# Second tiles moved straight behind gate and up, rows turned ahead of down, second rows always fetched

## The chip, the cores and the metric

The kernel runs on one core of one Trainium2 chip. The metric is the device time of one execution in microseconds (us); of several executions the median is given. TensorE (PE) does the matrix products and transposes, VectorE (DVE) and ScalarE (ACT) the element work, GpSimd (POOL) issues the gathers and the adding scatters, and SyncE (SP) issues most of the weight loads. DMA engines move data beside them.

## The reference

One encoder layer over 1024 tokens of width 1024: a token mixer (neighbourhood attention beside a bidirectional gated DeltaNet, one output projection), and then a mixture of 64 small experts. The change touches the experts alone. Each token chooses one of 8 groups and in it the 2 best of 8 experts; each expert's hidden width is 256.

```python
def expert_block(args):
    tok, e = args
    xb = h_pad[tok]
    hid = jax.nn.silu(xb @ w_gate[e]) * (xb @ w_up[e])
    return hid @ w_down[e]
...
out = (out.reshape(p_rows, d_).astype(jnp.float32) * buf_gate[:, None]).astype(h.dtype)
y = jnp.zeros((n + 1, d_), h.dtype).at[buf_tok].add(out)[:n]
```

All weights are float32: 2 MB for gate and up of one expert, 1 MB for down, 201 MB for all 64. Which tokens an expert gets is known only at run time.

## The kernel before, in words

The mixer, the router and the tables of rows take the first 840 us or so. The experts follow, in 32 steps of two experts each (e and e + 32). Each expert gives a first tile of up to 64 rows, so that a step fills 128 rows. An expert with more than 64 tokens has a second tile of up to 64 rows, which is computed only if it is there.

Step i of the loop (lines 1145 to 1168) consists of these pieces, written in this order:

- weights: `load_w` (L951, its DMA is L958) for the tiles that come free. There are 7 tiles of gate and up (`wg`) and 6 of down (`wd`). At step 0 these loads are on POOL's queue, later on SP's.
- `gather` (L1019) of the 128 rows of step i + 2 into one of three buffers `xg`, an indirect DMA issued by POOL (L1021). In this program's lists the three buffers are xg_8037, xg_8038 and xg_8039, for steps 0, 1 and 2, then 3, 4 and 5, and so on.
- `gate_up` (L1034): 16 products into `pp` on PE (L1041; the trace counts two matmuls for each, 32 in all), SiLU on ACT (L1044), the product with up on DVE into `sg` (L1045).
- the branch on the larger count of the two experts (L1155): when it is taken, the second rows `xs` are turned and one `second_tile` (L1081) is done for each expert that has one (inner branch L1159, its sum into the output is L1057 too).
- `second` (L1125) for the next step: its count is loaded into registers of all engines (L1127), and inside a branch of its own (L1128) the two gathers of second rows are issued.
- `finish(i - 1)`: `down` (L1066) of the step before: 8 products into `po` (L1076; 16 in the trace), the scaling on DVE (L1078), and an indirect DMA on POOL that adds the rows into the output (L1057).
- `turn_h` (L1048): two transposes of `sg`.
- `turn` (L1024) for the next step: 8 transposes of `xg` on PE (L1029), multiplied on DVE into `xT` (L1030).

A scheduler reorders the instructions of each engine within a stretch between two branches; it does not move them past a branch's ends. So what stands ahead of a branch in an engine's list stays ahead of it. The branch is decided by each engine for itself, from registers that it loads with TENSOR_LOAD. `reuse_waits="tile"` means that a tile's next writer waits for the last reader of the tile.

In this profile the branch L1155 is taken in 6 of the 32 steps, and 7 second tiles are done. The first is in step 0.

Of the kernel before, what the change touches and what calls it, by code (L numbers as in the profile page):

```python
# [8 lines left out]
F32 = mybir.dt.float32  # L9
# [10 lines left out]
P = 128  # L20
# [10 lines left out]
CAP = 64  # L31
# [5 lines left out]
def tile_layer(ctx, tc, a, out):  # L37
# [31 lines left out]
    def load_split(src, cols):  # L69
        hi = wpl.tile([P, NK, 256], F32R, name="w_hi")[:, :, :cols]  # L70
        lo = wpl.tile([P, NK, 256], F32R, name="w_lo")[:, :, :cols]
        for k in range(0, NK, 2):
            raw = wpl.tile([P, 2, 256], F32, name="w_raw")[:, :, :cols]
            sp.dma_start(raw, src[:, k:k + 2])
            act.activation(hi[:, k:k + 2], raw, AF.Copy)  # L75
            dve.tensor_sub(lo[:, k:k + 2], raw, hi[:, k:k + 2].bitcast(F32))  # L76
        return hi, lo
# [352 lines left out]
    ws = {b: load_split(a["w_nat"][b], 256) for b in border[:2]}  # L430
# [33 lines left out]
    with tc.tile_pool(name="ty", bufs=1, side="right") as ty:  # L464
        TT = ty.tile([P, NH, CH], F32, name="TT")
        XdT = ty.tile([P, NH, 32], F32, name="XdT")
        wt = ty.tile([P, NH, 32], F32, name="wt")
# [42 lines left out]
    for n in range(NCH):  # L510
# [3 lines left out]
        at, w = atb[n % 2], wb[n % 2]  # L514
# [450 lines left out]
    steps = [(gp, gp * 8 + j) for j in range(8) for gp in range(4)]  # L965
    wt = {}
    pace = [steps[i // 2][1] + 32 * (i % 2) for i in range(4)]
    for f, t in [(None, 0)] + tail:
        ins = f(t) if f else last
        if f is None or f is ao_mm and t in (4, 6, 7):  # L970
            e = pace.pop(0)
            wt.setdefault(e % 32, []).append(load_w(mwA, e, after=ins))
        if f is ao_mm and t == NT - 1:
# [5 lines left out]
            tS = [m1.tile([P, 32, 4], I32, name="tS"), m1.tile([CAP, 64, 4], I32, name="t2")]  # L979
            ln2p = m1.tile([P, NK], F32, name="ln2p")  # L980
            act.dma_start(ln2p, a["ln2"][:, 1])
            LA = 2
            xgb = [m1.tile([P, D], F32, name=f"xg{i}") for i in range(LA + 1)]
            xg2 = m1.tile([P, D], F32, name="xs")
# [31 lines left out]
    psX = ctx.enter_context(tc.tile_pool(name="psX", bufs=2, space=PSUM, reuse_waits="tile"))  # L1016
# [3 lines left out]
    def gather(xg, meta, n):  # L1020
        return pool.indirect_dma_start(out=xg[:n], out_offset=None, in_=x2_d, in_offset=bass.IndirectOffsetOnAxis(ap=meta[:n, 0:1], axis=0),  # L1021
                                bounds_check=S - 1, oob_is_err=False)

    def turn(xg, n):  # L1024
        xT = m2.tile([P, NK, P], F32, name="xT")
        for g in range(2):
            pt = psX.tile([P, 4, P], F32, name="pt")
            for k in range(4):
                pe.transpose(pt[:, k, :n], xg[:n, g * 4 + k:D:NK], ident[:n, :n])  # L1029
            dve.tensor_tensor(xT[:, g * 4:g * 4 + 4, :n], pt[:, :, :n],  # L1030
                              ln2p[:, g * 4:g * 4 + 4, None].to_broadcast([P, 4, n]), op=OP.mult)
        return xT

    def gate_up(ws, meta, xT):  # L1034

        n = CAP * len(ws)
        mf = meta.bitcast(F32)
        pp = psX.tile([P, 2, 256], F32, name="pp")
        for k in range(NK):
            for d in range(len(ws)):  # L1040
                pe.matmul(pp[d * CAP:(d + 1) * CAP], xT[:, k, d * CAP:(d + 1) * CAP],  # L1041
                          ws[d][0][:, :, k * 256:(k + 1) * 256], start=(k == 0), stop=(k == NK - 1))
        sg = m2.tile([P, 256], F32, name="sg")
        act.activation(sg[:n], pp[:n, 0], AF.Silu, scale=mf[:n, 3:4])  # L1044
        dve.scalar_tensor_tensor(sg[:n], pp[:n, 1], mf[:n, 3:4], sg[:n], op0=OP.mult, op1=OP.mult)  # L1045
        return sg

    def turn_h(sg, n):  # L1048
        ph = psX.tile([P, 2, P], F32, name="ph", bufs=1)
        for k in range(2):  # L1050
            pe.transpose(ph[:, k, :n], sg[:n, k:256:2], ident[:n, :n])  # L1051
        hT = m2.tile([P, 2, P], F32, name="hT")
        act.activation(hT[:, :, :n], ph[:, :, :n], AF.Copy)  # L1053
        return hT
# [12 lines left out]
    def down(ws, meta, hT, gp):  # L1067
        n = CAP * len(ws)
        mf = meta.bitcast(F32)
        yg = m2.tile([P, D], F32, name="yg", bufs=3)  # L1070
        for c in range(2):
            cs = slice(c * 512, (c + 1) * 512)
            po = psX.tile([P, 512], F32, name="po")
            for k in range(2):
                for d, w in enumerate(ws):
                    pe.matmul(po[d * CAP:(d + 1) * CAP], hT[:, k, d * CAP:(d + 1) * CAP],  # L1076
                              w[1][:, k * D + c * 512:k * D + (c + 1) * 512], start=(k == 0), stop=(k == 1))
            dve.tensor_scalar(yg[:n, cs], po[:n], mf[:n, 2:3], None, op0=OP.mult)  # L1078
        add_rows(yg[:n], meta[:n, 0:1], gp, (0, 1))

    def second_tile(w, d, meta, xT, gp):  # L1081

        hs = [slice(0, CAP), slice(CAP, 2 * CAP)]
        me, mine = hs[0], hs[d]
        mf = meta.bitcast(F32)
        pp = psX.tile([P, 2, 256], F32, name="pp")
        for k in range(NK):
            for i in range(2):
                pe.matmul(pp[hs[i], i], xT[:, k, mine], w[0][:, i, k * 256:(k + 1) * 256], start=(k == 0), stop=(k == NK - 1))
        sg = m2.tile([CAP, 256], F32, name="sg2", bufs=1)  # L1090
        act.activation(sg[:], pp[me, 0], AF.Silu, scale=mf[me, 3:4])
        dve.scalar_tensor_tensor(sg[:], pp[hs[1], 1], mf[me, 3:4], sg[:], op0=OP.mult, op1=OP.mult)
        ph = psX.tile([P, 2, P], F32, name="ph", bufs=1)
        for k in range(2):
            pe.transpose(ph[:, k, :CAP], sg[:, k:256:2], ident[me, me])
        hT = m2.tile([P, 2, CAP], F32, name="hT2", bufs=1)
        act.activation(hT, ph[:, :, :CAP], AF.Copy)
        yg = m2.tile([P, D], F32, name="yg", bufs=3)
        po = psX.tile([P, 512], F32, name="po")
        for k in range(2):  # L1100
            for c in range(2):
                pe.matmul(po[hs[c]], hT[:, k], w[1][:, k * D + c * 512:k * D + (c + 1) * 512],
                          start=(k == 0), stop=(k == 1))
        for c in range(2):
            dve.tensor_scalar(yg[me, c * 512:(c + 1) * 512], po[hs[c]], mf[me, 2:3], None, op0=OP.mult)
        add_rows(yg[me], meta[me, 0:1], gp, (d,))

    NS = len(steps)
# [14 lines left out]
    more, xTs = {}, {}  # L1123

    def second(i):  # L1125
        e = steps[i][1]
        more[i] = nc.values_load(ci[:, e:e + 1], min_val=0, max_val=S)  # L1127
        with tc.If(more[i] > CAP):  # L1128
            for d in range(2):
                gather(xg2[d * CAP:(d + 1) * CAP], tS[1][:, e + 32 * d], CAP)  # L1130

    for i in range(LA):
        ins = gather(xgb[i], tS[0][:, steps[i][1]], P)
    for i in placed[-2:]:
        tc.add_manual_dep(i.ins, ins.ins.name, mybir.DependencyInfo(mybir.DependencyClass.NoSync, mybir.DependencyReason.DATA),
                          reason="the first rows are more urgent")
    xTs[0] = turn(xgb[0], P)
    second(0)
    hTs = {}

    def finish(i):
        gp, e = steps[i]
        down(wt[e], tS[0][:, e], hTs.pop(i), gp)

    for i in range(NS):
        gp, e = steps[i]
        args = (pool, ins, mybir.DependencyClass.NoSync) if i == 0 else ()
        for n, part in upto(i):
            f = steps[n // 2][1]
            mw = mwA if n % room[part] < 4 else mwB if n % room[part] == 4 else (mwG, mwD)[part]  # L1150
            wt.setdefault(f, [[], []])[n % 2] += load_w(mw, f + n % 2 * 32, *args, parts=(part,))
        if i + LA < NS:
            gather(xgb[(i + LA) % (LA + 1)], tS[0][:, steps[i + LA][1]], P)
        sg = gate_up(wt[e], tS[0][:, e], xTs.pop(i))
        with tc.If(more[i] > CAP):  # L1155
            xT = turn(xg2, P)
            for d in range(2):
                c = nc.values_load(ci[:, 128 + e + 32 * d:129 + e + 32 * d], min_val=0, max_val=S)
                with tc.If(c > CAP):  # L1159
                    second_tile(wt[e][d], d, tS[1][:, e + 32 * d], xT, gp)  # L1160
        if i + 1 < NS:
            second(i + 1)
        if i > 0:
            finish(i - 1)
        hTs[i] = turn_h(sg, P)
        if i + 1 < NS:
            xTs[i + 1] = turn(xgb[(i + 1) % (LA + 1)], P)
    finish(NS - 1)
    rest = nc.values_load(ci[:, 32:33], min_val=0, max_val=S)  # L1169
    with tc.If(rest > 0):  # L1170
        with tc.For_i(0, 64) as e:
            left = nc.values_load(ci[:, bass.ds(e + 64, 1)], min_val=0, max_val=14)
            with tc.For_i(0, left) as i:
                w = load_w(mwA, e)
                meta = m2.tile([P, 4], I32, name="meta")
                sp.dma_start(meta[:CAP], tbl[bass.ds(e * S + i * CAP + 2 * CAP, CAP)])
                gather(xgb[0], meta, CAP)
                down([w], meta, turn_h(gate_up([w], meta, turn(xgb[0], CAP)), CAP), None)


def layout(inputs):
# [64 lines left out]
```

## Time and profile before

| | |
|---|---|
| median of 3 runs | 1406.26 us (1401.35 to 1408.34) |
| profiled execution, own time | 1408.78 us |
| its span in the trace | 1407.0 us (1.8 us lie around it) |
| mean granted TensorE clock | 0.944 |
| busy: PE, DVE, ACT, POOL | 85%, 47%, 28%, 28% of the span |
| experts stage | from about 842 us to the end |
| SP queue's weight loads | 62 of 2 MB, 63 of 1 MB |

Times in the trace count from the span's start. The trace's views used are: busy time of each engine in a chosen stretch (windows), instructions in order of time (timeline), the DMA queues' packets, one line's instructions, and the list of waits. In a timeline row the bracket at the end says how long the engine was idle before the instruction and what ended that idle time. An engine name with a q (PEq, DVEq, SPq) is that engine's sequencer, which runs branches and register loads. The DMA share of a window is the mean busy share of the 16 DMA engines; it can come out a little over 1.

### The profile page before, as it was taken

How to read it: one execution, taken by the hardware profiler on the slowest of the kernel's cores; microseconds unless marked ns; L12 is line 12 of the kernel's file. 1: busy time of each engine (PE TensorE's matmuls, PEld its weight loads, DVE VectorE, ACT ScalarE, POOL GpSimd, SP SyncE). 2: the span in 40 equal slices, each digit the busy share in tenths (PEclk: the TensorE clock that was granted, in tenths of full speed). 3: DMA queues.
4: the chain of work that ended last, by engine and by line, in shares of the span. 5: the costliest groups of instructions: out<-in, count | busy, mean ns of one | idle time of the engine just before them, and what ended most of it. 6: DMA issues, size and time to landing. Idle time of an engine off the chain costs nothing. (4 is left out here: it accounts for less than half of the span.)

```text
span 1407.0 us, 20840 instructions
## 1 busy us (share of the span) xinstructions
PE 1194.1 (85%) x7307; PEld 828.0 (59%) x7308; DVE 660.1 (47%) x1631; ACT 393.9 (28%) x800; POOL 387.4 (28%) x435
## 2 busy tenths in 40 slices
PE   6977999979999996688989968888887788878885
PEld 6866889969988895466768853333332333333332
DVE  5556853853667652667858871212211212222211
ACT  6435422322354441765445320000000000000000
POOL 1147313021655544112110242212212112211111
PEclk9989999989999997799999979999998899989998
DMA  4251246346565469998694788999999899998991
GB/s 158 71 114 42 75 135 177 94 138 148 166 176 148 119 172 221 297 262 206 169 216 165 285 332 323 397 404 401 400 406 394 352 387 407 395 364 331 402 379 38
DMA packets 109953, 347.11 MB, mean 247 GB/s; under 512 B 43104, under 2 KB 49248, under 8 KB 93168
## 3 DMA queue, kind: packets, MB, share of 16 engines
q1 hardware_dynamic: 74480, 260.68, 51.3%
q0 software_dynamic: 27056, 68.79, 19.0%
q10 hardware_dynamic: 8272, 15.78, 3.2%
q8 instruction: 82, 1.34, 0.4%
q14 instruction: 63, 0.52, 0.1%
HBM read 305.26 MB, written 61.67 MB: 261 GB/s over the span
## 5 line engine op out<-in xcount | busy, mean ns | idle before, releaser
L1041 PE MATMUL pp<-wg,xT 128*64 128x512 f32 x1024 | 233.1, 604 | 19.7 <-DVE xT L1030 19.4
L1041 PEld LDWEIGHTS pp<-wg,xT 128*64 128x64 f32 x1024 | 74.4, 139 | 156.4 <-issue 128.2
L1076 PE MATMUL po<-wd,hT 128*64 128x512 f32 x512 | 126.8, 622 | 45.1 <-DVEq L1155 28.3
L84 PE MATMUL pA<-w_hi,h_hi 128*128 128x256 f32 x512 | 151.1, 295 | 0.0
L86 PE MATMUL pA<-w_hi,h_lo 128*128 128x256 f32 x512 | 149.9, 293 | 0.0
L85 PE MATMUL pA<-w_lo,h_hi 128*128 128x256 f32 x512 | 149.9, 293 | 0.0
L1057 POOL DMA_INDIRECT out<-yg,tS x32 | 50.8, 1587 | 291.3 <-DVE yg L1078 242.8
L1045 DVE SCALAR_TENSOR_TENSOR sg<-pp,tS,sg 128x256 f32<-128x256 f32 x32 | 15.5, 484 | 233.2 <-ACTq L1155 189.0
L1076 PEld LDWEIGHTS po<-wd,hT 128*64 128x64 f32 x512 | 42.1, 142 | 129.5 <-issue 68.4
L1078 DVE TENSOR_SCALAR yg<-po,tS 128x512 f32<-128x512 f32 x64 | 47.0, 749 | 126.2 <-DMA out<-yg,tS 66.8
L84 PEld LDWEIGHTS pA<-w_hi,h_hi 128*128 128x128 f32 x512 | 100.5, 196 | 0.7 <-issue 0.2
L85 PEld LDWEIGHTS pA<-w_lo,h_hi 128*128 128x128 f32 x512 | 100.4, 196 | 0.2
L86 PEld LDWEIGHTS pA<-w_hi,h_lo 128*128 128x128 f32 x512 | 100.2, 196 | 0.3
L1044 ACT ACTIVATE sg<-pp,tS 128x256 f32<-128x256 f32 x32 | 15.2, 474 | 272.7 <-PE pp L1041 272.7
L84 PE MATMUL pA<-h_hi,w_hi 128*128 128x512 f32 x192 | 76.5, 398 | 0.0
L85 PE MATMUL pA<-h_lo,w_hi 128*128 128x512 f32 x192 | 76.4, 398 | 0.0
L86 PE MATMUL pA<-h_hi,w_lo 128*128 128x512 f32 x192 | 75.9, 395 | 0.0
L76 DVE TENSOR_TENSOR w_lo<-w_raw,w_hi 128x512 fp32r<-128x512 f32 x56 | 38.5, 702 | 71.1 <-ACT w_hi L75 69.4
L250 DVE SCALAR_TENSOR_TENSOR acc<-raw,convw,acc 128x1024 f32<-128x1024 f32 x48 | 63.2, 1320 | 12.4 <-ACT acc L248 11.9
L1053 ACT ACTIVATE hT<-ph 128x256 f32<-128x256 f32 x32 | 12.3, 384 | 191.6 <-PE ph L1051 191.6
L84 PE MATMUL pA<-wo_hi,t_hi 128*128 128x512 f32 x128 | 54.7, 427 | 9.3 <-ACT t_hi L750 6.9
L665 PE MATMUL pv<-pT,vw 128*128 128x256 f32 x192 | 55.2, 425 | 3.3 <-ACT pT L656 2.2
(340 smaller groups left out, 2422.4 us busy)
## 6 DMA issues: line engine op xcount, KB each, us to landing
wg<-in_w_gu SPq DMA_DIRECT2D x62, 2048.0 KB
wd<-in_w_down SPq DMA_DIRECT2D x63, 1024.0 KB
bt<-in_bias SPq DMA_DIRECT2D x24, 384.0 KB
w_raw<-in_w_nat SPq DMA_DIRECT2D x32, 256.0 KB
w_raw<-in_w_dn SPq DMA_DIRECT2D x24, 256.0 KB
k<-kk_d POOLq DMA_DIRECT2D x16, 384.0 KB
SA_d<-cm POOLq DMA_DIRECT2D x8, 512.0 KB
kk_d<-ev POOLq DMA_DIRECT2D x8, 512.0 KB
```

The lines of the kernel that those rows point to most:

```text
L76: dve.tensor_sub(lo[:, k:k + 2], raw, hi[:, k:k + 2].bitcast(F32))
L84: pe.matmul(dst, sh, mh, start=(i == 0), stop=False)
L85: pe.matmul(dst, sh, ml, start=False, stop=False)
L86: pe.matmul(dst, sl, mh, start=False, stop=(i == n - 1))
L250: dve.scalar_tensor_tensor(acc, raw[:, t:t + S], convw[:, m, t:t + 1], acc, op0=OP.mult, op1=OP.add)
L665: pe.matmul(pv, vw[:, w, half + g, pr * P:(pr + 1) * P], pT[:, g], start=(g == 0), stop=(g == 2))
L1041: pe.matmul(pp[d * CAP:(d + 1) * CAP], xT[:, k, d * CAP:(d + 1) * CAP], ws[d][0][:, :, k * 256:(k + 1) * 256], start=(k == 0), stop=(k == ...
L1044: act.activation(sg[:n], pp[:n, 0], AF.Silu, scale=mf[:n, 3:4])
L1045: dve.scalar_tensor_tensor(sg[:n], pp[:n, 1], mf[:n, 3:4], sg[:n], op0=OP.mult, op1=OP.mult)
L1057: ins = pool.indirect_dma_start(out=out, out_offset=bass.IndirectOffsetOnAxis(ap=idx, axis=0), in_=yg, in_offset=None, bounds_check=S - 1, ...
L1076: pe.matmul(po[d * CAP:(d + 1) * CAP], hT[:, k, d * CAP:(d + 1) * CAP], w[1][:, k * D + c * 512:k * D + (c + 1) * 512], start=(k == 0), st ...
L1078: dve.tensor_scalar(yg[:n, cs], po[:n], mf[:n, 2:3], None, op0=OP.mult)
```

## The change

`gate_up` now ends after the products; SiLU and the product with up are a new function `hidden`, written behind the branch. The second tile has a PSUM tile of its own, `p2`. The two gathers of second rows lose their branch and are issued in every step; where there are no second rows, the indexes lie out of bounds. The count is loaded by a function of its own, ahead of the next `gate_up`. The turn of the next rows is written ahead of `down`. Lines behind the edit move: the branch L1155 is now L1162, the inner branch L1159 is L1166, `pp` L1039, `sg` L1047, `ph` L1053, the adding scatter L1059, `po` L1078, the scaling L1080, the count's load L1134.

```diff
@@ -1033,13 +1033,15 @@
 
     def gate_up(ws, meta, xT):
 
-        n = CAP * len(ws)
-        mf = meta.bitcast(F32)
         pp = psX.tile([P, 2, 256], F32, name="pp")
         for k in range(NK):
             for d in range(len(ws)):
                 pe.matmul(pp[d * CAP:(d + 1) * CAP], xT[:, k, d * CAP:(d + 1) * CAP],
                           ws[d][0][:, :, k * 256:(k + 1) * 256], start=(k == 0), stop=(k == NK - 1))
+        return pp
+
+    def hidden(pp, meta, n):
+        mf = meta.bitcast(F32)
         sg = m2.tile([P, 256], F32, name="sg")
         act.activation(sg[:n], pp[:n, 0], AF.Silu, scale=mf[:n, 3:4])
         dve.scalar_tensor_tensor(sg[:n], pp[:n, 1], mf[:n, 3:4], sg[:n], op0=OP.mult, op1=OP.mult)
@@ -1083,7 +1085,7 @@
         hs = [slice(0, CAP), slice(CAP, 2 * CAP)]
         me, mine = hs[0], hs[d]
         mf = meta.bitcast(F32)
-        pp = psX.tile([P, 2, 256], F32, name="pp")
+        pp = psX.tile([P, 2, 256], F32, name="p2", bufs=1)
         for k in range(NK):
             for i in range(2):
                 pe.matmul(pp[hs[i], i], xT[:, k, mine], w[0][:, i, k * 256:(k + 1) * 256], start=(k == 0), stop=(k == NK - 1))
@@ -1123,11 +1125,13 @@
     more, xTs = {}, {}
 
     def second(i):
+
+        for d in range(2):
+            gather(xg2[d * CAP:(d + 1) * CAP], tS[1][:, steps[i][1] + 32 * d], CAP)
+
+    def count(i):
         e = steps[i][1]
         more[i] = nc.values_load(ci[:, e:e + 1], min_val=0, max_val=S)
-        with tc.If(more[i] > CAP):
-            for d in range(2):
-                gather(xg2[d * CAP:(d + 1) * CAP], tS[1][:, e + 32 * d], CAP)
 
     for i in range(LA):
         ins = gather(xgb[i], tS[0][:, steps[i][1]], P)
@@ -1136,6 +1140,7 @@
                           reason="the first rows are more urgent")
     xTs[0] = turn(xgb[0], P)
     second(0)
+    count(0)
     hTs = {}
 
     def finish(i):
@@ -1151,20 +1156,22 @@
             wt.setdefault(f, [[], []])[n % 2] += load_w(mw, f + n % 2 * 32, *args, parts=(part,))
         if i + LA < NS:
             gather(xgb[(i + LA) % (LA + 1)], tS[0][:, steps[i + LA][1]], P)
-        sg = gate_up(wt[e], tS[0][:, e], xTs.pop(i))
+        if i + 1 < NS:
+            count(i + 1)
+        pp = gate_up(wt[e], tS[0][:, e], xTs.pop(i))
         with tc.If(more[i] > CAP):
             xT = turn(xg2, P)
             for d in range(2):
                 c = nc.values_load(ci[:, 128 + e + 32 * d:129 + e + 32 * d], min_val=0, max_val=S)
                 with tc.If(c > CAP):
                     second_tile(wt[e][d], d, tS[1][:, e + 32 * d], xT, gp)
+        sg = hidden(pp, tS[0][:, e], P)
         if i + 1 < NS:
             second(i + 1)
+            xTs[i + 1] = turn(xgb[(i + 1) % (LA + 1)], P)
         if i > 0:
             finish(i - 1)
         hTs[i] = turn_h(sg, P)
-        if i + 1 < NS:
-            xTs[i + 1] = turn(xgb[(i + 1) % (LA + 1)], P)
     finish(NS - 1)
     rest = nc.values_load(ci[:, 32:33], min_val=0, max_val=S)
     with tc.If(rest > 0):
@@ -1175,7 +1182,8 @@
                 meta = m2.tile([P, 4], I32, name="meta")
                 sp.dma_start(meta[:CAP], tbl[bass.ds(e * S + i * CAP + 2 * CAP, CAP)])
                 gather(xgb[0], meta, CAP)
-                down([w], meta, turn_h(gate_up([w], meta, turn(xgb[0], CAP)), CAP), None)
+                pp = gate_up([w], meta, turn(xgb[0], CAP))
+                down([w], meta, turn_h(hidden(pp, meta, CAP), CAP), None)
 
 
 def layout(inputs):
```

On POOL, at the start of the experts stage, the list before goes from the gather of step 2's rows (xg_8039) to the two weight loads and the branch of step 0, which is taken:

```order
L1021 DMA xg_8039<-x_d,tS 128x1024
L958 DMA wg<-in_w_gu 128x4096 x2
L1155 COMPARE_AND_BRANCH
L1158 TENSOR_LOAD ci
L1159 COMPARE_AND_BRANCH
L1057 DMA out<-yg,t_8034 1024x1024
```

The list now, from the second rows of step 0 on (inside the branch, the rows of the second expert's tile are left out):

```order
L1021 DMA xs<-x_d,t_8034 64x1024 x2
L958 DMA wg<-in_w_gu 128x4096
L1134 TENSOR_LOAD ci
L1162 COMPARE_AND_BRANCH
L1165 TENSOR_LOAD ci
L1166 COMPARE_AND_BRANCH
L1059 DMA out<-yg,t_8034 1024x1024
...
L1162 UNCONDITIONAL_BRANCH
L958 DMA wg<-in_w_gu 128x4096
L958 DMA wd<-in_w_down 128x2048
L1021 DMA xg_8039<-x_d,tS 128x1024
```

One of the two loads of gate and up, and the gather of step 2's rows, moved from ahead of the branch to behind it, and the gather now stands behind a load of down as well.

On PE, at the same place, the list now divides the products of step 0 into 5 ahead of the branch and 11 behind it; before, all 16 stood ahead:

```order
L1029 MATMUL pt<-ident,xg_8037 128x128 x8
L1039 MATMUL pp<-wg,xT 64x512 x5
L1134 TENSOR_LOAD ci
L1162 COMPARE_AND_BRANCH
L1029 MATMUL pt<-ident,xs 128x128 x8
...
L1162 UNCONDITIONAL_BRANCH
L1039 MATMUL pp<-wg,xT 64x512 x11
L1029 MATMUL pt<-ident,xg_8038 128x128 x8
```

What moved is the second tile of step 0: it now runs before two thirds of its step's products.

Two steps on, PE's list now has the turn of step 2's rows ahead of the down products of step 0:

```order
L1162 UNCONDITIONAL_BRANCH
L1029 MATMUL pt<-ident,xg_8039 128x128 x8
L1078 MATMUL po<-wd,hT 64x512 x8
L1053 MATMUL ph<-ident,sg 128x128 x2
```

Before, `po` and `ph` stood first and the turn behind them. An ordinary step later in the loop has the same order, with 16 products `pp` and the branch behind these four rows.

On DVE, an ordinary step's list before, from one branch to the next:

```order
L1128 UNCONDITIONAL_BRANCH x2
L1078 TENSOR_SCALAR yg<-po,tS 128x512 x2
L1030 TENSOR_TENSOR xT<-pt,ln2p 128x512 x2
L1045 SCALAR_TENSOR_TENSOR sg<-pp,tS,sg 128x256
L1155 COMPARE_AND_BRANCH
```

and now:

```order
L1162 UNCONDITIONAL_BRANCH
L1030 TENSOR_TENSOR xT<-pt,ln2p 128x512 x2
L1080 TENSOR_SCALAR yg<-po,tS 128x512 x2
L1047 SCALAR_TENSOR_TENSOR sg<-pp,tS,sg 128x256
L1134 TENSOR_LOAD ci
L1162 COMPARE_AND_BRANCH
```

`xT` moved ahead of `yg`, the branch L1128 is gone, and `sg` still stands ahead of the branch, although the code has it behind.

## Rows read from the trace of the kernel before

**Rows 1.** Windows; columns: stretch, its length, each engine's busy us, clock, DMA

```profile
core 0: us, PE busy (x) PEld busy (x) DVE busy (x) ACT busy (x) POOL busy (x), PEclk, DMA share, GB/s
857.00:866.00 9.00, 6.45 (x46) 3.21 (x44) 2.46 (x5) 0.75 (x2) 0.00 (x0) 1.00 0.97 379
870.00:1100.00 230.00, 196.24 (x927) 77.97 (x925) 50.15 (x78) 13.23 (x31) 44.41 (x35) 0.97 1.01 400
1100.00:1130.00 30.00, 21.87 (x108) 9.44 (x106) 6.75 (x10) 1.88 (x5) 5.56 (x4) 0.83 0.88 336
1300.00:1360.00 60.00, 51.53 (x242) 19.82 (x240) 12.63 (x20) 3.43 (x8) 9.51 (x7) 0.97 1.01 400
1372.00:1386.00 14.00, 12.07 (x58) 4.78 (x58) 2.80 (x6) 0.86 (x2) 1.56 (x1) 1.00 0.21 68
```

**Rows 2.** Timeline of PE, two places where PE waits for weights

```profile
1061.76 5.29 PE L1076 MATMUL po<-wd,hT 128*64 128x512 f32 x14 [3.78 <-DMA wd<-in_w_down]
1254.94 3.68 PE L1102 MATMUL po<-wd,hT 128*64 128x512 f32 x8 [6.66 <-DMA wd<-in_w_down]
```

**Rows 3.** Timeline of POOL, start of the experts stage

```profile
849.55 1.02 POOL L1021 DMA_INDIRECT xg<-x_d,tS  x1 [0.30 <-issue]
850.58 1.18 POOL L958 DMA_DIRECT2D wg<-in_w_gu  x2
...
867.36 1.54 POOL L1057 DMA_INDIRECT out<-yg,t  x1 [15.61 <-DVEq L1159]
```

**Rows 4.** Timeline of PE, start of the experts stage

```profile
848.41 7.89 PE L1041 MATMUL pp<-wg,xT 128*64 128x512 f32 x32
856.24 1.16 PE L1029 MATMUL pt<-ident,xs 128*128 128x128 f32 x8
...
863.58 1.94 PE L1102 MATMUL po<-wd,hT 128*64 128x512 f32 x8 [0.37 <-ACT hT L1097]
...
868.22 7.76 PE L1041 MATMUL pp<-wg,xT 128*64 128x512 f32 x32 [0.77 <-DVE xT L1030]
```

**Rows 5.** Timeline of SP, its first loads of gate and up here

```profile
861.72 14.72 SPq L958 DMA_DIRECT2D wg<-in_w_gu  x3
```

**Rows 6.** DMA queues (packets, MB, share), 1222 to 1246 us

```profile
q1 hardware_dynamic: 752, 8.03, 85.1%
q0 software_dynamic: 702, 0.89, 15.6%
```

**Rows 7.** DMA queues, 848.5 to 851 us: two gathers of second rows

```profile
q0 software_dynamic: 160, 0.10, 19.3%
```

**Rows 8.** DMA queues, 1392 to 1397 us: one operation of 128 rows

```profile
q0 software_dynamic: 144, 0.10, 16.9%
```

**Rows 9.** Waits of PE from 1254 us to the end (us, count, longest)

```profile
PE po L1076 <- DVEq L1155: 7.2, 6, 1.2
PE pp L1041 <- DVE xT L1030: 5.8, 7, 2.3
```

**Rows 10.** Timeline of all engines, DVE's and PE's rows of an ordinary step

```profile
1357.38 0.48 DVE L1045 SCALAR_TENSOR_TENSOR sg<-pp,tS,sg 128x256 f32<-128x256 f32 x1 [7.10 <-ACTq L1155]
...
1358.02 3.65 PE L1076 MATMUL po<-wd,hT 128*64 128x512 f32 x16 [1.20 <-DVEq L1155]
```

**Rows 11.** Lines L1127 on PE, L1155 and L1021 on POOL (ns: least/mean/most)

```profile
L1127 PEldq TENSOR_LOAD <-ci x32: 297/303/488, 846.0 to 1372.2; - x32
L1155 POOLq INC_SWDGE_SEM x26: 714/1275/2046, 875.7 to 1377.9; - x26
L1021 POOL DMA_INDIRECT xs<-x_d,t x12: 939/952/984, 847.0 to 1265.6; - x12
```

**Rows 12.** Timeline of all engines, the adding scatter and the buffer it frees

```profile
1204.48 1.58 POOL L1057 DMA_INDIRECT out<-yg,tS  x1 [10.97 <-DVE yg L1078]
...
1216.07 1.54 DVE L1078 TENSOR_SCALAR yg<-po,tS 128x512 f32<-128x512 f32 x2 [3.09 <-DMA out<-yg,tS]
...
1217.89 1.58 POOL L1057 DMA_INDIRECT out<-yg,tS  x1 [10.46 <-DVE yg L1078]
```

## The prediction

> **What bounds the kernel now.** I first read the windows by stage. From 870 to 1100 us the DMA engines are fully busy at 400 GB/s, and PE has work for 196 of 230 us [rows 1]: the weights set the pace. A step needs 6.29 MB of them (two loads of 2 MB, two of 1 MB) and some 0.5 MB of rows in and out, by 0.400 MB/us an estimated 17.0 us. PE does a step in less: 58 matmul rows are a step, and the window from 1300 to 1360 us has 242, so 60 / (242/58) = 14.4 us. PE therefore catches up and then waits for weights, 3.78 us before one down at 1061 us and 6.66 us at 1254.94 us [rows 2]. The DMA engines rest only where PE is late after a taken branch and holds the tiles: 12% of 30 us from 1100 on, 3.6 us [rows 1]. Behind 1254.94 us PE no longer starves: the last steps' weights arrive until about 1372 us (share 0.21 behind it [rows 1]), and PE's own steps end the program. So a DMA engine that idles early is paid in full, unless PE's last seven steps give it back.
>
> **The start.** Before, POOL issues both first loads of gate and up in 1.18 us, ahead of the branch of step 0 [rows 3]. They feed the DMA engines until SP's first load of gate and up at 861.72 us [rows 5], which waits for tiles of step 0; between 857 and 866 us the engines are 97% busy [rows 1]. Now only one of the two stands ahead of the branch. At 388 to 400 GB/s its 2.1 MB take 5.2 to 5.4 us; the issue ends near 851.2, so data that flows from about 852 us ends at about 857 us. The next loads wait behind step 0. PE does 5 of 16 products, 5/16 x 7.89 = 2.5 us from 848.41, so to 850.9 us; then the second tile, 865.52 - 856.24 = 9.3 us [rows 4], to 860.2, with half a microsecond for the branch's end 860.7; then 11 products, 5.4 us, to 866.1. That releases step 0's tiles for SP, 4.4 us later than 861.72. POOL leaves the branch after the scatter, which before was issued 1.84 us behind the last product (865.52 to 867.36) and took 1.54 [rows 3, 4]: now about 862.5 + 1.5 = 864, and its load flows a little over a microsecond later. So the engines idle from 857 to 866: 9 us x 0.97 = **+8.7**. Bounds: 5, if PE or POOL is 4 us sooner, and 10.
>
> **The rows of step 2.** Their gather stood ahead of the loads at 849.55 us [rows 3]. Now it is behind POOL's second load of gate and up and its load of down, in the same queue. That queue and SP's take turns by packets: 752 against 702 where both had work, 702/24 = 29.25 a microsecond [rows 6]. POOL's 2.1 MB beside SP's 2.1 MB: 10.5 us, to 876.5; POOL's 1.05 MB, whose packets I take as half as big, beside another 2.1 MB of SP: 7.9 us, to 884.4; then the gather's 144 packets (the count of one 128-row operation [rows 8]) at 29.25 each microsecond: 4.9 us, to 889.3. PE would have finished step 1's products 8.9 us behind 866.1 (a turn of 1.16 and 7.76 [rows 4]), at 875. By PE's new order the down of step 0 stands behind the turn of step 2's rows, so PE idles from 875 to 889, and down ends at 889.3 + 1.16 + 3.65 [rows 4, 10], 894 to 895.5. Only then does a tile of down come free for SP, whose gate and up queued before ends near 890.2. The engines idle again, **+5.3**; bounds 0 (the rows come before 875) and 6.5.
>
> **PE's order.** With the turn ahead of down, xT is made while PE does down, and the wait of the products for xT goes: 5.8 us over 7 steps behind 1254 us [rows 9]. I take six sevenths, **-5.0**, because the step at 1254.94 starved for weights anyway [rows 2]; earlier steps gain only in the two rests of the DMA engines. Of the first, 3.6 us, I take **-1.5** (0 to -3.6). The ends for the last stretch: 0, if xT's place is taken by another wait, and -11.5, if besides xT most of the 7.2 us in front of down went.
>
> **The wait in front of down** (1.20 us in an ordinary step, six in the last stretch [rows 9, 10]) I leave. PE waits for DVE's part of the branch, which stands behind sg; on DVE sg still stands ahead of the branch, so only the name of the waiting instruction changes, from down to the turn. Down starts at 1358.02, 0.16 us after sg ends at 1357.86 [rows 10]. In front of it stood the jump over L1155, the count's load (303 ns on PE [rows 11]), a compare and the jump over L1128: all that beside sg. So the removed branch and the earlier load of the counts are worth 0 to -0.16 x 6 = -1.0; I take **0**.
>
> The Trainium skill, page "Runtime: NRT & Kernel Launch", section "Instruction fetch mechanics", says that a taken branch to a place outside the two pages at hand makes the engine fetch the page before it goes on; it gives no price. By it each of the 26 jumps over L1128 that the change removes would have stopped an engine, and the whole 7.2 us could go, which would give 1407. The trace speaks against it here: 0.16 us is all that is left behind sg for two jumps and a load.
>
> **Gathers in every step.** 12 gathers become 64: 52 more, each 952 ns of POOL in place of the semaphore steps of 1.3 us in 26 skipped branches [rows 11]; POOL is far from full (9.5 of 60 us [rows 1]), so **0**; bounds 0 and, if their packets decide, +7.3 (below). On POOL's queue a step has now 80 + 80 packets of second rows (160 for two [rows 7]; I take absent rows to cost the same) and twice 144: 448 / 29.25 = 15.3 us. That is below 17.0, so hidden while the weights decide.
>
> **Sum**: 8.7 + 5.3 - 5.0 - 1.5 = +7.5 on 1408.8, the profiled execution's own time: 1416.3. It was 2.5 above the median of the runs shown, so I predict **1414**, 0.55% above it. A measurement of this kernel can tell about 0.5% from no change: below 1399.2 is faster, above 1413.3 slower.
>
> **Rivals.** (a) Faster: PE's last steps decide more than I grant. The first hole at its low end, 5, no second, the rest of the DMA engines and the last stretch in full: 1408.8 + 5 - 3.6 - 11.5 - 2.5 = 1396. For it: PE is the bound behind 1255. Against: sg ahead of the branch on DVE keeps most of the 7.2. 10%.
>
> (b) No change: the rows of step 2 arrive before 875, because the packets of rows are small (0.89 MB in 702, 1.3 KB each, against 10.7 KB [rows 6]) and the loads' are taken faster than by turns. No second hole, and the rest in full: 8.7 - 5.0 - 3.6 = 0.1: 1406. Against: that queue served 29.25 packets a microsecond and no more. 28%. Here belongs also that the branch is cheaper than it looks (1407, above).
>
> (c) Slower: POOL's queue becomes the bound of the last steps. The scatter frees the buffer that a later `yg` waits for, already 3.09 us, and scatters follow each other at 13.4 us (1204.48 to 1217.89) [rows 12]. If now 15.3 us a step is the least, it decides from the point where PE would do a step faster, 14.4: 0.9 x 8 steps from 1255 to 1372, +7.3, and the -5.0 doesn't come: 1413.8 + 12.3 = 1426. For it: yg's waits. Against: behind the last weights the queue has no rival, and absent rows may cost less. 20%.
>
> **Chances.** The forecast has 42%, with its own range of 1408 to 1420. Half of it lies below 1413.3. Faster: (a) and a little, 0.12. Same: (b) mostly, and 0.18 of the forecast, 0.42. Slower: (c), half of the forecast and the upper side of (b), 0.46. The range of 1400 to 1427 holds (b), the forecast and (c), and leaves out most of (a).
>
> **What would show it.** Right: DMA share near zero from 857 to 866; PE idle before the turn of step 2's rows until near 889, and a second, shorter rest of the DMA engines behind it; last weights 12 to 14 us later than 1372; no wait for xT in ordinary steps, but 1.2 us before the turn, from DVE's branch. Wrong: the first hole filled by the second load, a tail shorter by more than 6 us from the last load to the end, steps spaced by scatters at 15 us, or ordinary steps without the wait behind sg.

## The result: slower by 1.1%

The changed kernel takes 1422.78 us (median of 4 runs, 1420.18 to 1424.14), the kernel before 1407.3 (1401.35 to 1409.54): a ratio of 1.0112, 95% interval 1.0088 to 1.0137, some 15.5 us. The forecast was 1414, in a range of 1400 to 1427. The profiled execution has a span of 1422.0 us against 1407.0.

The start of the experts stage, first as windows of the changed kernel (columns as in [rows 1]; the first of them answers to the first row there):

```profile
857.00:866.00 9.00, 8.24 (x40) 2.93 (x36) 2.29 (x4) 1.76 (x2) 4.04 (x5) 1.00 0.30 63
866.00:876.00 10.00, 8.47 (x34) 2.65 (x34) 1.38 (x3) 0.86 (x2) 2.60 (x3) 1.00 0.99 420
876.00:890.00 14.00, 0.58 (x3) 0.61 (x4) 0.00 (x0) 0.00 (x0) 0.00 (x0) 0.59 0.89 370
890.00:897.00 7.00, 7.00 (x24) 2.48 (x22) 2.14 (x3) 0.00 (x0) 3.87 (x4) 0.60 0.19 45
```

The kernel before, in the last two of these windows:

```profile
876.00:890.00 14.00, 12.07 (x58) 4.68 (x58) 3.27 (x5) 1.14 (x3) 2.66 (x2) 1.00 1.00 369
890.00:897.00 7.00, 4.99 (x26) 2.48 (x26) 1.83 (x4) 0.58 (x2) 0.00 (x0) 1.00 1.02 395
```

From 857 to 866 us the DMA engines are 30% busy where they were 97% [rows 1], and from 890 to 897 they are 19% busy where they were full. Between the two PE does 0.58 us of work in 14 us. The same stretch in the changed kernel's timelines of PE, of POOL and of SP:

```profile
846.24 3.56 PE L1039 MATMUL pp<-wg,xT 128*64 128x512 f32 x10
849.72 1.16 PE L1029 MATMUL pt<-ident,xs 128*128 128x128 f32 x8
...
859.16 5.36 PE L1039 MATMUL pp<-wg,xT 128*64 128x512 f32 x22 [0.43 <-PEq L1166]
...
889.42 1.94 PE L1029 MATMUL pt<-ident,xg 128*128 128x128 f32 x8 [14.95 <-DMA xg<-x_d,tS]
891.29 5.78 PE L1078 MATMUL po<-wd,hT 128*64 128x512 f32 x16
```

```profile
847.48 0.62 POOL L958 DMA_DIRECT2D wg<-in_w_gu  x1
860.58 1.54 POOL L1059 DMA_INDIRECT out<-yg,t  x1 [12.47 <-DVEq L1166]
862.90 0.59 POOL L958 DMA_DIRECT2D wg<-in_w_gu  x1 [0.78 <-issue]
863.48 0.56 POOL L958 DMA_DIRECT2D wd<-in_w_down  x1
864.34 1.05 POOL L1021 DMA_INDIRECT xg<-x_d,tS  x1 [0.30 <-issue]
```

```profile
863.72 11.21 SPq L958 DMA_DIRECT2D wg<-in_w_gu  x3
897.10 0.33 SPq L958 DMA_DIRECT2D wd<-in_w_down  x1
```

These answer to [rows 3 to 5]. The two loads of gate and up that POOL issued within 1.18 us are now 15.4 us apart, SP's first load comes 2.0 us later, and the gather of step 2's rows, issued at 864.34, lets PE go on only at 889.42. The next load of down is issued at 897.10, behind the down that waited for that turn.

An ordinary step of the last stretch, changed kernel, timeline of all engines; it answers to [rows 10]:

```profile
1331.05 0.47 ACT L1046 ACTIVATE sg<-pp,tS 128x256 f32<-128x256 f32 x1 [6.58 <-PE pp L1039]
...
1331.73 1.41 DVE L1080 TENSOR_SCALAR yg<-po,tS 128x512 f32<-128x512 f32 x2 [10.88 <-DMA out<-yg,tS]
1333.05 0.48 DVE L1047 SCALAR_TENSOR_TENSOR sg<-pp,tS,sg 128x256 f32<-128x256 f32 x1
...
1333.69 1.13 PE L1029 MATMUL pt<-ident,xg 128*128 128x128 f32 x8 [2.69 <-DVEq L1162]
```

The wait for xT is gone, but PE's wait behind the products has grown from 1.20 to 2.69 us: `yg` waits for the scatter of the step before until 1331.73, later than the products' end, and sg and the branch stand behind `yg` on DVE. The waits of the changed kernel from the stage's start to the end, total, count, longest (before, 66.8 us in 18 for `yg`, and 28.3 in 23, at most 1.7, for PE in front of down):

```profile
DVE yg L1080 <- DMA out<-yg,tS: 172.6, 20, 11.8
...
PE pt L1029 <- DVEq L1162: 37.0, 19, 3.6
```

At the end the weights run out some 20 us later than before, as two windows, the kernel before and then the changed one, show:

```profile
1370.00:1372.00 2.00, 0.96 (x6) 0.08 (x2) 0.48 (x1) 0.47 (x1) 0.00 (x0) 1.00 0.59 215
1390.00:1392.00 2.00, 2.00 (x12) 1.17 (x12) 0.75 (x2) 0.47 (x1) 1.00 (x2) 1.00 0.75 213
```

The span ends only 15.0 us later: some 5 us less lie behind the last weights.

### The profile page after: what moved, and what is told of

Read it like the earlier page. It is cut to its first block, busy times and chain, and to the rows that moved or that the text cites. A ratio compares the mean times of both kernels' runs of the same rounds, so it can differ in the third digit from the quotient of the medians.

```text
span 1422.0 us, 20690 instructions
## 1 busy us (share of the span) xinstructions
PE 1208.3 (85%) x7307; PEld 829.8 (58%) x7308; DVE 660.7 (46%) x1631; ACT 395.1 (28%) x801; POOL 433.7 (30%) x487
## 5 line engine op out<-in xcount | busy, mean ns | idle before, releaser
L1039 PE MATMUL pp<-wg,xT 128*64 128x512 f32 x1024 | 240.3, 604 | 7.0 <-DMA wg<-in_w_gu 5.0
L1039 PEld LDWEIGHTS pp<-wg,xT 128*64 128x64 f32 x1024 | 74.2, 139 | 148.3 <-issue 136.1
L1080 DVE TENSOR_SCALAR yg<-po,tS 128x512 f32<-128x512 f32 x64 | 46.1, 748 | 206.6 <-DMA out<-yg,tS 172.6
L1078 PE MATMUL po<-wd,hT 128*64 128x512 f32 x512 | 125.6, 623 | 2.8 <-DMA wd<-in_w_down 1.2
L1059 POOL DMA_INDIRECT out<-yg,tS x32 | 51.3, 1604 | 189.3 <-DVE yg L1080 163.8
L1029 PE MATMUL pt<-ident,xg 128*128 128x128 f32 x256 | 39.4, 301 | 64.2 <-DVEq L1162 37.0
L1021 POOL DMA_INDIRECT xs<-x_d,t x64 | 61.2, 956 | 100.0 <-PE pt L1029 34.1
L1029 PEld LDWEIGHTS pt<-ident,xg 128*128 128x128 f32 x256 | 33.3, 196 | 91.2 <-issue 75.3
L1030 DVE TENSOR_TENSOR xT<-pt,ln2p 128x512 f32<-128x512 f32 x76 | 49.6, 687 | 63.2 <-PE pt L1029 60.4
L1078 PEld LDWEIGHTS po<-wd,hT 128*64 128x64 f32 x512 | 36.6, 142 | 68.3 <-issue 60.4
```

What stands on the lines that cost most here:

```text
L1059: ins = pool.indirect_dma_start(out=out, out_offset=bass.IndirectOffsetOnAxis(ap=idx, axis=0), in_=yg, in_offset=None, bounds_check=S - 1, ...
```

## The experiments

Two theories stood against each other. **Start**: the loss is the DMA engines' idle time at the start. **Packets**: the second rows gathered in every step lengthen the scatters on POOL's queue, and an early rest would be made up. Times are medians; the ratio to the kernel before, measured on the same chip, stands behind with its interval. Differences between two versions go by these ratios, since the kernel before measured 1405 to 1407 us from one group of runs to the next; 0.1% is 1.4 us. The first four kernels ran against a before of 1405.9, the next four against 1406.2.

**e1, the second tile's PSUM tile shared again**

```diff
-        pp = psX.tile([P, 2, 256], F32, name="p2", bufs=1)
+        pp = psX.tile([P, 2, 256], F32, name="pp")
```

> The changed kernel (1422.8 us) with one edit undone: the second tile takes its PSUM tile from the two pp buffers again. The order then has all 16 products of step 0 and both loads of gate and up ahead of its branch; the gather of step 2's rows stays behind a load of down. Theory 'start': the weights lost about 15 us of DMA time at the start, some 6.5 because one load stood behind the branch and some 8 because step 2's rows stood behind two loads; with one load of down ahead of the rows, the second part shrinks to about 3. Expected 1410 to 1417 us, DMA share over 0.9 from 857 to 866, PE still idle 3 to 6 us before the turn of step 2's rows. Rival 'packets': the second rows gathered in every step lengthen the scatters, and any rest at the start would be made up: 1420 to 1424 us.

1410.97, ratio 1.0042 (1.0028 to 1.0056). One line takes back 0.70%, some 9.8 us of the 15.7 that the ratio 1.0112 of the changed kernel stands for. PE's wait for step 2's rows, in the timeline of PE, falls from 14.95 to 3.68 us:

```profile
876.51 1.13 PE L1029 MATMUL pt<-ident,xg 128*128 128x128 f32 x8 [3.68 <-DMA xg<-x_d,tS]
```

A miss inside it: the share from 857 to 866 was 0.85, not over 0.9. In this profile the first loads are issued 3.5 us earlier (847.06), so they are likely to run dry earlier too.

**e2, as e1, and step 2's rows ahead of the loads**

```diff
+    gather(xgb[LA], tS[0][:, steps[LA][1]], P)
...
-        if i + LA < NS:
+        if 0 < i < NS - LA:
```

> As the run before it, and the gather of step 2's rows is issued ahead of the first loads, as in the kernel before. Nothing of the start is then changed; the gathers in every step and the turn ahead of down stay. Theory 'start': 1405 to 1410 us, no idle time of PE before the turn of step 2's rows and the last weights at about 1385 us as in the kernel before. Rival 'packets': 1418 to 1424 us, with a normal start and lag that grows from step to step.

1406.12, ratio 1.0007 (0.9991 to 1.0023). The rest of the loss is gone, 4.9 us more; the turn of step 2's rows waits for no rows:

```profile
874.96 1.13 PE L1029 MATMUL pt<-ident,xg 128*128 128x128 f32 x8 [1.65 <-DVEq L1163]
```

So the start costs 1.0112 - 1.0007, some 14.8 us (the bare medians, each beside another measurement of the kernel before, give 16.7), and the gathers in every step together with the turn ahead of down cost nothing that can be measured. Theory "packets" falls as the main cause of the loss; that the two parts are not nothing each, but offset each other, e3 and e4 show.

**e3, the turn ahead of down alone, on the kernel before**

```diff
+            xTs[i + 1] = turn(xgb[(i + 1) % (LA + 1)], P)
         if i > 0:
             finish(i - 1)
         hTs[i] = turn_h(sg, P)
-        if i + 1 < NS:
-            xTs[i + 1] = turn(xgb[(i + 1) % (LA + 1)], P)
```

> The kernel before (1407 us) with the next rows' turn written ahead of down, and nothing else of the change. The forecast's own term says 1401 (5.0 from the last stretch and 1.5 from the rests). Theory 'start' with the scatter's buffer as the limit: xT's wait goes, but yg's wait for the scatter now stands between xT and sg on DVE and delays sg and the branch, so most of the gain is taken back: 1403 to 1407. Rival: no scatter limit, 1396 to 1401.

1404.14, ratio 0.9991 (0.9975 to 1.0007): between a gain of 3.5 us and a loss of 1.0. PE's waits for xT vanish from the last stretch and the wait behind the products stays, as its list of waits from 1254 us on shows:

```profile
PE pt L1029 <- DVEq L1155: 7.2, 6, 1.2
PE pt L1029 <- DMA xs<-x_d,t: 3.8, 1, 3.8
```

The time is what theory "start" gave, but not by its mechanism: it had `yg` delay the branch, and the wait behind the products is 1.2 us here, as long as in the kernel before. Why the vanished wait for xT brings so little is open.

**e4, the gathers in every step alone, on the kernel before**

```diff
-        with tc.If(more[i] > CAP):
-            for d in range(2):
-                gather(xg2[d * CAP:(d + 1) * CAP], tS[1][:, e + 32 * d], CAP)
+        for d in range(2):
+            gather(xg2[d * CAP:(d + 1) * CAP], tS[1][:, e + 32 * d], CAP)
```

(and step 2's rows ahead of the loads, by e2's edit)

> The kernel before with the second rows gathered in every step and without the branch for them, the start's order kept (step 2's rows ahead of the loads). Theory 'start': the gathers lie below the weights' time, and only the last stretch pays through longer scatters: 1407 to 1412. Rival 'packets': 1417 to 1423, the whole loss of the changed kernel. By the forecast: no change, 1405 to 1408.

1407.83, ratio 1.0020 (1.0001 to 1.0038): a cost of about 2.8 us, 0.1 to 5.3. The cost shows in the weights. In the kernel before they have thinned out 523.6 us behind the first product of step 0: the DMA engines are 21% busy from 1372 to 1386 us [rows 1]. The same 14 us, counted from each run's own first product (844.34, 847.00 and 844.79 us), of e3, e4 and e2:

```profile
1367.94:1381.94 14.00, 12.05 (x54) 5.94 (x52) 2.06 (x4) 1.24 (x3) 1.56 (x1) 1.00 0.25 83
1370.60:1384.60 14.00, 12.39 (x62) 4.82 (x60) 3.33 (x6) 0.86 (x2) 4.02 (x4) 1.00 0.48 175
1368.39:1382.39 14.00, 12.72 (x62) 4.70 (x60) 4.59 (x7) 0.86 (x2) 3.49 (x3) 1.00 0.50 181
```

With the gathers in every step the weights end some 4 us later (0.27 x 14), an estimate from one profile of each. The later runs agree: e6, e9 and e10, which gather in every step, have 0.49, 0.44 and 0.55 there, e7 and e8, which don't, 0.22 and 0.18. As e2 takes no longer than the kernel before, what else it has of the change, the turn ahead of down above all, gives about as much back behind the last weights.

**e5, a PSUM tile of its own alone, on the kernel before** (e1's edit the other way round)

> The kernel before with one edit of the change alone: the second tile's PSUM tile of its own. The order then has 1 product of step 0 and one load of gate and up ahead of its branch; step 2's rows stay ahead of both loads. Theory 'start': only the first rest of the DMA engines (857 to 866 us) comes, 6 to 9 us, so 1411 to 1415. Rival: the idle time is made up by the end, 1405 to 1408.

1423.03, ratio 1.0120 (1.0101 to 1.0139). The direction is theory "start"'s, the size is not: 8 us more than its upper end. The profile shows one more place. With the branch free to stand early, the fetch of the second rows on POOL comes straight in front of it, and at the taken branch near 1295 us PE waits for them. PE's row:

```profile
1295.66 1.94 PE L1029 MATMUL pt<-ident,xs 128*128 128x128 f32 x8 [12.47 <-DMA xs<-x_d,t]
```

The rows were asked for at 1278.80 and 1280.07 us. While PE waits it frees no weight tiles, and the DMA engines rest as well, for some 12 us in these two windows, where the kernel before lost 5.6 us around its taken branches there (0.14 of the 40 us from 1260):

```profile
1285.00:1295.00 10.00, 0.00 (x0) 0.00 (x0) 0.00 (x0) 0.00 (x0) 0.00 (x0) 0.54 0.47 185
1295.00:1305.00 10.00, 7.82 (x46) 4.88 (x48) 1.87 (x3) 0.74 (x2) 0.00 (x0) 0.77 0.31 103
```

In the changed kernel the rows are fetched in every step, and its longest wait for them in the last stretch is 4.0 us. That this rest is the 8 us is likely from one profile and was not tried by itself.

**e6 to e8, the scatter's buffers divided**, in the same memory: of the three `yg` two for first tiles and one for second tiles. e6 is e2 with it, e7 the kernel before with it, e8 is e3 with it. The first place is in `down`, the second in `second_tile`.

```diff
-        yg = m2.tile([P, D], F32, name="yg", bufs=3)
+        yg = m2.tile([P, D], F32, name="yg", bufs=2)
...
-        yg = m2.tile([P, D], F32, name="yg", bufs=3)
+        yg = m2.tile([P, D], F32, name="yg2", bufs=1)
```

> Run e2 (1406.1 us) with the scatter's buffers divided: two yg for first tiles, one for second tiles, the same memory, so that yg of a step no longer waits for the scatter of the step before. Theory 'buffer': PE's waits before the turn fall from 2.7 to 1.2 us, yg's waits for the scatter (208.7 us) nearly vanish; where PE decides (after 1255 us) 6 steps of 1.5 us are gained and the rests of the DMA engines shrink: 1396 to 1401. Rival 'packets': the queue itself is the limit, whichever buffer is free: 1404 to 1408.

> The kernel before with the buffers divided alone. yg's waits (66.8 us) vanish; xT behind it on DVE comes sooner, so part of xT's 5.8 us in the last stretch goes. Theory 'buffer': 1400 to 1404. Rival, the weights decide all but the tail: 1405 to 1408.

> The kernel before with the turn ahead of down and the buffers divided. Theory 'buffer': the wait before the turn was 1.2 us already without the divided buffers, so little is added to e3 (1404.1): 1398 to 1403, the fastest of all. Rival: as e3, 1403 to 1406, since the last weights bound the end.

1404.82, 1405.96 and 1402.73; ratios 0.9991 (0.9979 to 1.0004), 1.0007 (0.9993 to 1.0020) and 0.9990 (0.9973 to 1.0006). None can be told from the kernel before, so e6 and e7 miss what theory "buffer" gave; e8's median is inside the range of that theory, but not told apart from its rival's. The mechanism itself showed: in e6's list of PE's waits from 1254 us on, the wait behind the products is back at 1.3 us on average, where e2 had 10.6 us in 6. But the second rows of taken branches now come late:

```profile
PE pt L1029 <- DMA xs<-x_d,t: 10.8, 2, 7.8
PE pt L1029 <- DVEq L1163: 7.8, 6, 1.4
```

**e9 and e10, the order that the code asks for.** Edges that set the order alone, with no semaphore: the branch behind the last product and, at step 0, behind both loads; SiLU behind the branch. e9 has the scatter's buffers as they were, e10 has them divided. Both have e2's early gather and the second tile's own PSUM.

```diff
+                if xg is xg2 and g == k == 0:
+                    tc.add_manual_dep(tr.ins, edge[-1].ins.name, ...)
+                    if len(edge) == 1:
+                        for w in issued[-3:-1]:
+                            tc.add_manual_dep(tr.ins, w.ins.name, ...)
+                    edge.append(tr)
...
+        sl = act.activation(sg[:n], pp[:n, 0], AF.Silu, scale=mf[:n, 3:4])
+        tc.add_manual_dep(sl.ins, edge[-1].ins.name, ...)
```

> The changed kernel with its intended order forced by ordering edges: step 2's rows and both first loads of gate and up ahead of step 0's branch, the branch behind all products, and SiLU and sg behind the branch on ACT and DVE. The scatter's buffers as they were. Theory 'buffer': on DVE yg now stands in front of the branch, and yg waits for the scatter of the step before, so PE's wait before the turn stays, near 1 to 2.5 us; 1402 to 1407. Rival 'sg': it was only sg that held the branch; the wait falls under 0.4 us and the time to 1394 to 1400.

> As e9, and the scatter's buffers divided as in e6. Theory 'buffer' and 'sg' agree: neither sg nor a scatter stands in front of the branch, PE's wait before the turn falls under 0.4 us, an ordinary step in the last stretch takes 13 us in place of 14.4: 7 to 9 us in the last stretch and up to 3 in the DMA engines' rests, 1393 to 1400. Rival, the weights decide all but the tail: the wait goes and the time stays, 1401 to 1405.

Against a before of 1406.6: 1403.30, ratio 0.9987 (0.9971 to 1.0002), and 1400.62, ratio 0.9960 (0.9943 to 0.9977). e10 is the fastest version here, 0.4% under the kernel before; it stops just above its expected range. The turn in ordinary steps of e9 and of e10, timelines of PE:

```profile
1312.92 1.94 PE L1032 MATMUL pt<-ident,xg 128*128 128x128 f32 x8 [3.02 <-DVEq L1176]
...
1328.71 1.05 PE L1032 MATMUL pt<-ident,xg 128*128 128x128 f32 x8 [0.64 <-PEq L1176]
```

```profile
1306.77 1.13 PE L1032 MATMUL pt<-ident,xg 128*128 128x128 f32 x8 [0.46 <-PEq L1176]
...
1319.39 1.13 PE L1032 MATMUL pt<-ident,xg 128*128 128x128 f32 x8 [0.46 <-PEq L1176]
```

In e10 the turns are 12.6 us apart, against 14.4 a step before, and PE is busy for 57.5 of the 60 us in which it had 51.5 [rows 1]:

```profile
1300.00:1360.00 60.00, 57.53 (x278) 21.75 (x276) 14.87 (x23) 3.91 (x9) 21.55 (x19) 1.00 1.02 402
```

In e9 some steps have it too, but where `yg` is late for the scatter the wait is 3.02 us: both theories hold, each for its part. The largest wait that is left to PE in e10 is that for second rows at taken branches, from 890 to 1254 us and from 1254 us on:

```profile
PE pt L1032 <- DMA xs<-x_d,t: 25.5, 2, 14.6
```

```profile
PE pt L1032 <- DMA xs<-x_d,t: 14.1, 2, 10.8
```

**e11, as e10, the second rows fetched in a branch again**, held by an edge right behind the branch of the step before (the count's load goes back with it)

```diff
+        with tc.If(more[i] > CAP):
+            for d in range(2):
+                got.append(gather(xg2[d * CAP:(d + 1) * CAP], ...))
...
+                if xg is not xg2 and g == k == 0 and got:
+                    tc.add_manual_dep(tr.ins, got[-1].ins.name, ...)
```

> As e10 (1400.6 us), but the second rows are fetched inside a branch on the count again, placed by ordering edges directly behind the branch of the step before. 52 gathers and 4160 packets go, a second branch on all engines comes back. In e10 PE waited 39.6 us in 4 places for second rows that came late in the queue. Theory 'packets': with fewer packets ahead of them the rows of a taken step come in time, the waits fall under 10 us, and 3 to 6 us are gained: 1394 to 1398. Rival 'branch': the second branch costs each ordinary step 0.3 us or more in front of the turn and the rows are no sooner: 1400 to 1404.

1401.71, ratio 0.9980 (0.9964 to 0.9996) against a before of 1404.8: by its time the rival's range. By the waits each theory is half right. The second rows are in time (PE's waits from 1254 us on), but PE waits 1.2 us in each ordinary step again, for sg:

```profile
PE pt L1032 <- DVE sg L1062: 6.9, 6, 1.2
PE pt L1032 <- DMA xs<-x_d,t: 2.9, 1, 2.9
```

The times of e10 and e11 can't be told apart, and the pair does not price the packets, since e11's start differs too: from 866 to 876 us its DMA engines rest for about 3 us, where e10 has a share of 0.98.

```profile
866.00:876.00 10.00, 8.99 (x33) 2.65 (x32) 1.14 (x2) 0.47 (x1) 2.06 (x2) 0.81 0.70 275
```

## Why the prediction held, and where it did not

The two terms of the start carried the forecast, and they are what the runs show. The other terms failed: the forecast was +7.5 us and the kernels measured lie 15.5 apart, and nearly all of the 8 us between them is the -6.5 of PE's order, set beside 0 for the gathers. e2, which has both and the old start, is at +1.0 (-1.3 to +3.2). That 1422.8 still lies in the range is in part luck: its upper end is the time of rival (c), whose step of 15.3 us did not come.

- **First rest, +8.7.** Right in its place and its cause: one load ahead of the branch, the engines dry from 857 to 866. Share lost there: (0.97 - 0.30) x 9 = 6.0 us. The stage began 2.2 us earlier in this profile (products from 846.24, before from 848.41 [rows 4]), and POOL's first load was issued 3 us earlier, so the engines also ran dry sooner: from 842 to 857 their share is 0.51, before 0.54, where 2.2 us more of work were due. That makes 6.0 + 0.5 + 2.2, some 8.7 us, an estimate; the agreement with +8.7 is closer than these windows can vouch for.
- **Second rest, +5.3.** The forecast had PE wait until 889.3 for step 2's rows; it waited until 889.42. So close an agreement is luck: the loads ahead of those rows began some 2 us sooner than forecast (SP's first at 863.72, not 866.1) and took as much longer. The rest behind it was longer: about 7.3 us by the two windows from 876 to 897, against full engines in the kernel before. The term that was too small is the price of the turn and of down behind the wait. I took 1.16 and 3.65 us; they took 1.94 and 5.78. PE had worked for 0.58 of 14 us, and the granted clock was 0.59 and 0.60 in these windows, near the lower of its two levels (1.2 of 2.4 GHz).
- Together 14.0 forecast; by the ratios e1 and e2 give 9.8 + 4.9, some 14.8. e1's line also moves step 2's rows by one load, so the two runs don't divide at the same point as the two terms.
- **PE's order, -5.0 and -1.5.** This is the first step that failed. xT's wait did go, as forecast, but e3 measures -1.3 (-3.5 to +1.0) in place of -6.5. The -1.5 has no sign at all: from 1100 to 1130 us e3's DMA share is 0.89, where it was 0.88. For the -5.0 there is a sign, though the times don't bear it out in full: the changed kernel has some 5 us less behind its last weights, and e3's one profile, its fastest execution, has 4.9 us less from the first product to the end. Against the gain worked in the changed kernel that `yg` with its wait for the scatter now stands between xT and sg, and the wait behind the products, which I left at 1.20 us, is 1.9 us on average. The working named that wait as a buffer's (rival c) and did not follow it to the new order on DVE.
- **Gathers in every step, 0.** This is the second. The absent rows do cost packets as I took them to, 80 a gather: POOL's queue has 4160 more packets, and 52 x 80 is 4160. The price is not 0 but about 2.8 us (e4). The working weighed the queue's 15.3 us against the 17.0 of a step and called the packets hidden while the weights decide; but the weights are what they delay, by some 4 us over the stage (e4 and e2 against e3). The forecast's "last weights 12 to 14 us later" became some 20. The queues of both kernels over the whole span (before, then changed; packets, MB, share):

```profile
q0 software_dynamic: 27056, 68.79, 19.0%
```

```profile
q0 software_dynamic: 31216, 68.81, 19.2%
```

- **Rivals.** (a) and (b) asked for no second rest; it came. (c) is seen in part: scatters lie 14.4 us apart (1333.42 to 1347.85 in the changed kernel's timeline, 13.4 before [rows 12]), below the 15.3 reckoned, and e2 shows that with the turn's gain beside it this costs no measurable time. The wait on DVE's branch stayed because sg stood in front of it, and here `yg` too: e9 takes it away where `yg` is not late, e10 in all ordinary steps.
- The Trainium skill's rule on branches ("Runtime: NRT & Kernel Launch", "Instruction fetch mechanics") stops an engine only at a jump out of the two pages at hand, and gives no price; no row shows where these jumps lead. The stall that the working drew from it did not show: e4 is without that branch, and PE still waits 8.0 us in 6 in front of down from 1254 us on, where the kernel before waits 7.2 in 6 [rows 9].

One sentence about the kernel was wrong. The text on the kernel before has the scheduler move nothing past a branch's ends. It does move single instructions past a branch, and the branch as a whole past them: 11 products and a load that the code has ahead of step 0's branch stood behind it. What held the branch back in the kernel before was a buffer that the second tile shared with the products. e1 and e5 show that line's effect in both directions.

## What to carry to other kernels

A shared buffer can be what keeps an order: before giving a branch's work a buffer of its own, look at what the scheduler then puts behind that branch, the first loads and gathers above all. A few microseconds of an idle weight stream at the start were paid nearly in full here (14.8 us by the runs, some 16 by the windows), and a wait saved on PE did not pay them back. Two edits that come out at nothing together may be a cost and a gain: price each alone, and look at where the stream ends and not only at the total. When an operation is moved ahead of another on an in-order engine, follow the wait of the one that is now in the middle to whatever stands behind it.

## What the runs showed of the hardware that was not expected

A gather of 64 rows whose indexes are out of bounds still makes its 80 packets, though it moves almost no bytes: 52 such gathers added 4160 packets and 0.02 MB. And a small gather behind large loads in one queue is as late as they are: 25 us from its issue at 864.34 to PE's start at 889.42, against 8.5 us in e1 (868.01 to 876.51), where one load of down stood ahead of it.
